# Gate scattering by products of float32r parts instead of whole float32 products, in one layer of a hybrid encoder

## The chip, the cores and the metric

The kernel runs on one core of a Trainium2 chip. The metric is the device time of one execution in microseconds (us), from profiled and timed executions on the chip; lower is better.

## What is computed

One layer over 512 tokens of width 1024, in float32, taken as four blocks of 128 tokens. A projection of the normalised tokens feeds two groups of heads: latent attention (8 heads) and a recurrent RWKV-7 group (8 heads). Their outputs go through an output projection and are added to the tokens. Then comes the part that matters here, a retrieval over 16384 single-neuron experts, each with a row u and a row v of 1024 numbers:

```python
q = (hb @ w_pq).reshape(TOK_BLOCK, PEER_HEADS, 2, PEER_DHALF)
s = jnp.einsum('thpd,hpnd->thpn', q, sub_keys)          # two halves, 128 keys each
s1, i1 = lax.top_k(s[:, :, 0], 16); s2, i2 = lax.top_k(s[:, :, 1], 16)
...                                                     # best 16 of the 256 sums
gate = jax.nn.softmax(top_s, axis=-1)                   # expert index = i1 * 128 + i2
act = jax.nn.gelu(jnp.einsum('thkd,td->thk', expert_u[idx], hb))
out = jnp.einsum('thk,thkd->td', gate * act, expert_v[idx])
```

Every token has 8 heads of 16 experts, so 128 slots, each with i1, i2 and a gate.

## The kernel before

**Stages.** The first 750 us hold the layer's mixing part, in lanes of stages that run side by side, and for each block a stage `back`: output projection (`out_proj`, L784), normalisation (`norm_ffn`, L801), key scores and best 16 (`retrieve`, L837) and the list of experts with its gates (`route`, L862). Blocks 1 and 2 are routed together, block 3 last.

**Experts in two ways.** Blocks 0 and 3 are *gathered* (`experts`, L969): for each of the 128 slots an indirect DMA fetches one row of u or v per token into one of four buffers `ga`, and VectorE multiplies it (L988 for u, L991 for v): 128 u steps and 128 v steps per block, 512 in all. Block 3's steps need the `idx` tile that block 3's `route` writes in L960. Blocks 1 and 2 are *dense* (`dense`, L1052): for their 256 tokens the core goes through all 128 tiles of 128 experts. `up(e)` multiplies the tokens by a tile of u and applies gelu; `down(e)` multiplies the activations by the gates (L1134) and then by a tile of v, adding into four PSUM banks for all 128 tiles (L1138 with whole float32 products, L1149 with float32r parts).

**Gates.** `down` needs the gates as a dense table `G`: for each i2 (partition), token and i1 one number. `gate_half` (L1028) makes it for one half of the i1 values at a time, in 32 iterations of 8 tokens. Slots lie on the partitions. Per iteration VectorE writes B, a one-hot of i1 (L1035), and multiplies it by the gates (L1036); ScalarE writes A, a one-hot of i2 (8 instructions in L1039, one in L1040); TensorE multiplies A by B, 8 products of 128x128 by 128x64 (L1043); ScalarE copies the result into `G` (L1048). B has four buffers, tag "x", which the v halves of L1146 share; A has two. The first half is made before `down(0)`, with the 16 calls `up(12)` to `up(27)` emitted between its iterations; all 32 iterations write into each part of `G`, so `down(0)` follows the last. The second half is emitted between `down(48)` and `down(63)`, two iterations per tile. Tiles run 16 ahead in `up`, in a fixed set of activation buffers; `up(28)` reuses the room of earlier tiles.

**Splitting.** `split` (L1061) makes two float32r tiles of a float32 tile: ScalarE copies it (L1063) and VectorE subtracts the copy (L1064). Some of u and v is split, the rest goes through whole float32 products.

**Memory and order.** `dense` closes the stack `last`, which holds the pools `wb` and `psb` of the `back` stages, and opens the pool `d2` on the same side, so in the room that `wb` gives back:

```python
    last.close()
    d2 = ctx.enter_context(tc.tile_pool(name="d2", bufs=1, side="right", reuse_waits="tile"))
```

In the kernel before, the first tiles of `d2` to be written are `dh` and `dl`, the split tokens, for `up(28)`; then its halves of u (`uh`, `ul`). A scheduler decides the order of the instructions on each engine from the order in which they are emitted and from what each depends on; every engine then runs its instructions strictly in that order. The `back` stages are emitted before `dense`, and the gathers after it.

Of the kernel before, what the change touches and what calls it, by code (L numbers as in the profile page):

```python
# [35 lines left out]
# columns of the packed per-channel vectors  # L36
# [7 lines left out]
# columns of the packed per-feature rows  # L44
# [6 lines left out]
# candidate pairs (a, b) of the two sorted lists that can be among the best 16 sums, in order of a * 16 + b:  # L51
# (a, b) has (a + 1) * (b + 1) - 1 pairs before it that are at least as large
# [3 lines left out]
# lanes of stages: buffers, banks and weight tiles (count, width) of each  # L56
# [7 lines left out]
# blocks whose tokens gather their experts' rows, blocks that go through all experts  # L64
# [4 lines left out]
# dense blocks: gates of HALF * 128 experts at a time, in GBUFS tiles of SUB * 128; activations run AHEAD tiles ahead,  # L69
# FIRST of them before the first gates, KEPT more wait in DRAM  # L70
# [6 lines left out]
def u_whole(e):  # L77
    """float32 products of four passes, where the vector engine has no time to split; else three exact parts"""
    return e < 28 or 47 <= e - AHEAD < 64
# [7 lines left out]
def layer_kernel(ctx: ExitStack, tc: tile.TileContext, x, pos, cvec, rvec, w_mla, w_rwkv, w_uq, w_ukv, lora, g2,  # L87
# [5 lines left out]
    # what the last block's tail needs lies apart: its pools outlive those of the other stages  # L93
# [4 lines left out]
    # the tail takes over the buffers of the second lane  # L98
# [41 lines left out]
    # ---------------------------------------------------------------- constants  # L140
# [65 lines left out]
    # rows (beta s | kappa s), columns (alpha t | rho t)  # L206
# [52 lines left out]
    # rotary tables, token-major  # L259
# [50 lines left out]
    def square_sum(src, scr, acc):  # L310
        """the squares go to a tile that is written after them"""
        act(scr, src, AF.Square, accum_out=acc)

    def head_squares(src, n, acc, h0=0):
        """acc[:, h0 + i] = sum of squares of src[:, i, :n]"""
        for i in range(src.shape[1]):
            act(sb([P, QK], "hscr", dt=BF16)[:, :n], src[:, i, :], AF.Square, accum_out=acc[:, h0 + i:h0 + i + 1])

    # ---------------------------------------------------------------- stages
    def norm_in(xt, hT, carry):  # L320
        """channel-major normalized tokens, after the last one of the block before"""
        ss = sb([P, 1], "ss", 2)
        square_sum(xt.rearrange("p (a b) -> p a b", a=KC), hT[:, :, 1:], ss)
        r = rstd(ss, 1, 1.0 / D, EPS, "nx")
        act(xt, xt, AF.Copy, scale=r)
        if carry is None:
            V.memset(hT[:, :, 0:1], 0.0)
        else:
            V.tensor_copy(hT[:, :, 0:1], carry)
        for i in range(2):  # L330
            p = bank()
            for j in range(4):
                nc.tensor.transpose(p[:, j * P:(j + 1) * P], xt[:, (4 * i + j) * P:(4 * i + j + 1) * P], ident)
            for j in range(4):
                act(hT[:, 4 * i + j, 1:P + 1], p[:, j * P:(j + 1) * P], AF.Copy, scale=col("g_mix", 4 * i + j))
            yield
        carry = sb([P, KC, 1], "carry", 2)
        V.tensor_copy(carry, hT[:, :, P:P + 1])
        return carry

    def rwkv_in(b, hT):
        pm = {}
        if b == EARLY:
            # the gather's buffers are idle until the first block's experts are known
            t = [gb([P, D], "ga", GA).rearrange("p (a b) -> p a b", b=P) for _ in range(2)]
            pm = {"k": t[0][:, 0:4], "r": t[0][:, 4:8], "v": t[1][:, 0:4], "x": t[1][:, 4:6]}
        for g, cols in (("x", (12, 13)), ("k", range(4, 8)), ("r", range(4)), ("v", range(8, 12))):
            if b != EARLY:
                pm[g] = sb([P, 4, P], "pm", PM, pool=wa) if len(cols) == 4 else sb([P, 2, P], "px", 2, pool=wa)
            for i, c in enumerate(cols):  # L350
                w = wtile(w_rwkv[c])
                p = bank()
                for kc in range(KC):
                    mm(p[:, :P + 1], w[:, kc, :], hT[:, kc, :], start=kc == 0, stop=kc == KC - 1)
                t = pm[g][:, i, :]
                act(t, p[:, 1:P + 1], AF.Copy, scale=ommu[:, c:c + 1])
                V.scalar_tensor_tensor(t, p[:, 0:P], col("mu", c), t, op0=OP.mult, op1=OP.add)
                yield
        return pm

    def mla(b, hT, yT):
# [31 lines left out]
        # queries  # L393
# [32 lines left out]
        # keys and values  # L426
# [27 lines left out]
        # block-causal attention, four heads at a time  # L454
# [73 lines left out]
    def rwkv_chunks(b, pm):  # L528
# [68 lines left out]
        # bonus weight and gate  # L597
# [8 lines left out]
        # values, token-major  # L606
# [17 lines left out]
        # chunk-local products  # L624
# [12 lines left out]
        # inverse of the unit lower triangular systems: two chunks stacked on the partitions, heads side by side  # L637
# [70 lines left out]
    def rwkv_scan(b, AR, BKt, MT, UV, YF, wc, bv, sg, yT):  # L708
        # the recurrence over chunks
# [48 lines left out]
        # group norm, bonus, gate  # L758
# [65 lines left out]
    def top16(items):  # L824
        """items: (values, indices, source); the chains of several items interleaved"""
# [11 lines left out]
    def retrieve(bs, h2T):  # L837
        """the best TOPK of both halves' keys, per block"""
# [23 lines left out]
    def route(b, tv, ti):  # L862
        yield
        # the lists of indices as steps: what each rank adds to the one before
# [31 lines left out]
        # rank a of the first list from a candidate's place, rank b of the second from its place within the run  # L896
# [130 lines left out]

    def gate_half(dn, g, parts):  # L1028
        """gates of experts i1 * 128 + i2, i1 in one half: [i2, sub, token, i1 of the SUB]; parts: what takes each run
        of subs"""  # L1030
        i1T, i2T, gT = slots
        for t0 in range(0, nd, 8):
            B = dn.tile([P, 8 * HALF], F32, tag="x", name=f"B{g}_{t0}", bufs=XB)
            B = B.rearrange("p (a b) -> p a b", a=8)
            V.tensor_tensor(B, bm(iotap[:, g * HALF:(g + 1) * HALF], 8), bc(i1T[:, t0:t0 + 8], HALF), op=OP.is_equal)  # L1035
            V.tensor_tensor(B, B, bc(gT[:, t0:t0 + 8], HALF), op=OP.mult)  # L1036
            A = dn.tile([P, 8, P], F32, tag="A", name=f"A{g}_{t0}", bufs=2)
# [4 lines left out]
            for j in range(8):  # L1042
                mm(p[:, j * HALF:(j + 1) * HALF], A[:, j, :], B[:, j, :], start=True, stop=True)  # L1043
# [8 lines left out]
    def dense():  # L1052
# [5 lines left out]
        d2 = ctx.enter_context(tc.tile_pool(name="d2", bufs=1, side="right", reuse_waits="tile"))  # L1058
        nt = len(DENSE)

        def split(t, hi, lo):  # L1061
            """two parts of a float32 tile that the one-pass products carry whole"""
# [13 lines left out]
        # room for activations in the buffers of the second lane  # L1076
# [14 lines left out]
        def up(e, keep=False):  # L1091
            """activations of the experts of a tile, for all tokens of these blocks"""
# [91 lines left out]
    # stages of the blocks, emitted in the order in which they would run side by side; what runs in one lane shares  # L1184
    # its buffers
# [101 lines left out]
```

## Time and profile before

| | |
|---|---|
| median of 3 runs | 1783.02 us (1781.82 to 1790.86) |
| span of the profiled execution, first to last instruction | 1781.3 us |
| TensorE matmul busy | 1651.5 us, 93% |
| VectorE busy | 1334.4 us, 75% |
| ScalarE busy | 932.6 us, 52% |
| GpSimd busy | 702.6 us, 39% |

PE is TensorE's matmul row and PEld its weight loads, DVE is VectorE, ACT ScalarE, POOL GpSimd, SP the engine that issues most DMAs. Matmuls overlap one another, so the duration of one is longer than the distance from its start to the next start; rates below are worked out from starts. The span is 1.7 us below the median of the runs; no other time of the profiled execution is given.

### The profile page before, as it was taken

Reading aid. Unit: us, or ns where it says so; the run is one execution under the profiler, and the core shown is the slowest. Engines: PE = TensorE matmul, PEld = TensorE weight load, DVE = VectorE, ACT = ScalarE, POOL = GpSimd, SP = SyncE. Lnnn points to the kernel's source line nnn. Section 1 sums busy time; section 2 is a strip of 40 time slices with the busy share of each in tenths; the row PEclk is TensorE's granted clock in tenths of the full one; section 3 lists DMA queues with packets and bytes.
Section 4 is the critical chain, followed back from the end, with each engine's and each line's share of the span. In section 5 each row is a group of like instructions: output and inputs, shape, how many; then the busy total and the mean of one; then the engine's idle time right before and its main releaser. Section 6 shows DMA issues by size and latency. Waiting matters only on the chain. (4 is left out here: it accounts for less than half of the span.)

```text
span 1781.3 us, 29137 instructions
## 1 busy us (share of the span) xinstructions
PE 1651.5 (93%) x10183; PEld 1394.3 (78%) x10183; DVE 1334.4 (75%) x2987; ACT 932.6 (52%) x2465; POOL 702.6 (39%) x562
## 2 busy tenths in 40 slices
PE   7999999998999998788997899999999999999987
PEld 6897799787867987567995577888777778888864
DVE  3412414775586789887789789998887799999898
ACT  5656454644545332367774334444768645445443
POOL 1001100244554444454443253334455446356453
PEclk9998999997697999988999999999989999999999
DMA  7634565596689988789997799998989999999988
GB/s 272 196 122 135 164 233 194 203 337 223 213 309 329 324 321 294 290 283 310 364 331 250 258 359 352 359 355 325 327 312 319 312 343 351 366 318 371 346 293 330
DMA packets 154866, 520.71 MB, mean 292 GB/s; under 512 B 17312, under 2 KB 24096, under 8 KB 154720
## 3 DMA queue, kind: packets, MB, share of 16 engines
q0 software_dynamic: 73728, 268.47, 43.1%
q1 hardware_dynamic: 80992, 250.39, 39.6%
q8 instruction: 80, 1.31, 0.3%
q14 instruction: 66, 0.54, 0.1%
HBM read 508.96 MB, written 9.83 MB: 291 GB/s over the span
## 5 line engine op out<-in xcount | busy, mean ns | idle before, releaser
L978 POOL DMA_INDIRECT ga<-in_expert_v_dram,idx x256 | 352.3, 1376 | 381.7 <-DVE acc L991 285.5
L978 POOL DMA_INDIRECT ga<-in_expert_u_dram,idx x256 | 299.8, 1171 | 372.0 <-DVE ga L988 257.5
L991 DVE SCALAR_TENSOR_TENSOR acc<-ga,dots,acc 128x1024 f32<-128x1024 f32 x256 | 327.9, 1281 | 65.9 <-DMA ga<-in_expert_v_dram,idx 64.9
L988 DVE SCALAR_TENSOR_TENSOR ga<-ga,h 128x1024 f32<-128x1024 f32 x256 | 311.6, 1220 | 52.3 <-DMA ga<-in_expert_u_dram,idx 52.1
L1149 PE MATMUL po<-xh,t 128*128 128x512 f32 x880 | 307.7, 407 | 12.7 <-DVE t L1064 5.7
L1117 PE MATMUL ps<-dh,ul 128*128 128x256 f32 x664 | 191.1, 288 | 7.9 <-DVE ul L1064 7.4
L1149 PEld LDWEIGHTS po<-xh,t 128*128 128x128 f32 x880 | 159.6, 192 | 48.6 <-ACT xh L1063 13.2
L1117 PE MATMUL ps<-dh,uh 128*128 128x256 f32 x664 | 189.8, 286 | 6.5 <-ACT uh L1063 6.5
L1149 PE MATMUL po<-xl,t 128*128 128x512 f32 x440 | 179.6, 408 | 14.6 <-DVE xl L1064 14.2
L1117 PE MATMUL ps<-dl,uh 128*128 128x256 f32 x664 | 187.5, 282 | 0.0
L1063 ACT ACTIVATE xh<-v 128x512 fp32r<-128x512 f32 x220 | 134.6, 626 | 96.4 <-PE po L1149 73.9
L1103 PE MATMUL ps<-t,u 128*128 128x256 f32 x720 | 172.6, 393 | 9.1 <-DMA u<-in_expert_ut_dram 8.8
L1103 PEld LDWEIGHTS ps<-t,u 128*128 128x128 f32 x720 | 138.5, 197 | 32.3 <-issue 6.3
L1064 DVE TENSOR_TENSOR xl<-v,xh 128x512 fp32r<-128x512 f32 x220 | 147.7, 690 | 16.2 <-ACT xh L1063 15.7
L1043 PEld LDWEIGHTS ps<-B,A 128*128 128x128 f32 x1024 | 131.3, 204 | 35.3 <-ACT ge L951 10.6
L1039 ACT ACTIVATE A<-iotap,slots 128x128 f32<-128x128 f32 x512 | 156.1, 395 | 0.0
L1043 PE MATMUL ps<-B,A 128*128 128x64 f32 x1024 | 131.5, 285 | 23.6 <-DVE B L1036 10.4
L1063 ACT ACTIVATE uh<-u 128x512 fp32r<-128x512 f32 x166 | 98.5, 625 | 83.8 <-PE ps L1117 52.0
L1117 PEld LDWEIGHTS ps<-dh,ul 128*128 128x128 f32 x664 | 126.4, 190 | 17.3 <-DVE ul L1064 13.4
L1117 PEld LDWEIGHTS ps<-dh,uh 128*128 128x128 f32 x664 | 126.4, 190 | 17.1 <-ACT uh L1063 10.0
L1117 PEld LDWEIGHTS ps<-dl,uh 128*128 128x128 f32 x664 | 126.4, 190 | 3.5 <-issue 0.7
L848 PE MATMUL ps<-h2T,wst 128*128 128x128 f32 (+1 forms) x768 | 125.1, 318 | 3.1 <-DMA wst<-in_w_pq_dram 3.1
(402 smaller groups left out, 2924.1 us busy)
## 6 DMA issues: line engine op xcount, KB each, us to landing
u<-in_expert_ut_dram SPq DMA_DIRECT2D x128, 512.0 KB, 6.7
v<-in_expert_v_dram SPq DMA_DIRECT2D x128, 512.0 KB, 6.6
wst<-in_w_rwkv_dram SPq DMA_DIRECT2D x56, 512.0 KB, 4.4
wst<-in_w_pq_dram SPq DMA_DIRECT2D x48, 512.0 KB, 6.7
wst<-in_w_o_dram SPq DMA_DIRECT2D x24, 512.0 KB, 5.2
wst<-in_w_mla_dram SPq DMA_DIRECT2D x16, 336.0 KB, 3.9
t<-in_x_dram SPq DMA_DIRECT2D x8, 512.0 KB, 4.6
wst<-in_w_ukv_dram SPq DMA_DIRECT2D x16, 256.0 KB, 3.5
```

The source lines that it names most:

```text
L848: mm(p[:, :nb * P], w[:, kc, :], h2T[:, kc, :], start=kc == 0, stop=kc == KC - 1)
L978: G.indirect_dma_start(out=t, out_offset=None, in_=table, in_offset=bass.IndirectOffsetOnAxis(ap=idx[:, j:j + 1], axis=0))
L988: V.scalar_tensor_tensor(u, u, 1.0, h2, op0=OP.mult, op1=OP.mult, accum_out=dots[:, j:j + 1])
L991: V.scalar_tensor_tensor(acc, row_of(expert_v, j), dots[:, j:j + 1], acc, op0=OP.mult, op1=OP.add)
L1039: act(A[:, j, :], iotap, AF.Abs, scale=-1.0, bias=i2T[:, t0 + j:t0 + j + 1])
L1043: mm(p[:, j * HALF:(j + 1) * HALF], A[:, j, :], B[:, j, :], start=True, stop=True)
L1063: act(hi, t, AF.Copy)
L1064: V.tensor_tensor(lo, t, hi, op=OP.subtract)
L1103: mm(p, u[:, kc, :], hd[kc // 2][:, kc % 2, :], start=kc == 0, stop=kc == KC - 1)
L1117: mm(p, a[:, k, :], h[:, kc, :], start=kc + i == 0, stop=kc == KC - 1 and i == 2)
L1149: mm(po[i][n], ww[:, i * P:(i + 1) * P], vv, start=e + k == 0, stop=e == P - 1 and k == 2)
```

## The change

The gates are split once, at the first call of `gate_half`, into two float32r tiles of 128x256 in the pool `d2`. Per iteration there are two tiles B: VectorE writes the one-hot of i1 into one of them and multiplies it by the high and by the low part. A and both B are float32r, and each of the 8 products becomes two, accumulated in PSUM. The other lines of the diff remove comments.

```diff
+    gparts = []
+
     def gate_half(dn, g, parts):
         i1T, i2T, gT = slots
+        if len(gparts) == 0:
+            gparts.extend(pools["d2"].tile([P, nd], F32R, name=f"g{n}") for n in "hl")
+            act(gparts[0], gT, AF.Copy)
+            V.tensor_tensor(gparts[1], gT, gparts[0], op=OP.subtract)
         for t0 in range(0, nd, 8):
-            B = dn.tile([P, 8 * HALF], F32, tag="x", name=f"B{g}_{t0}", bufs=XB)
-            B = B.rearrange("p (a b) -> p a b", a=8)
-            V.tensor_tensor(B, bm(iotap[:, g * HALF:(g + 1) * HALF], 8), bc(i1T[:, t0:t0 + 8], HALF), op=OP.is_equal)
-            V.tensor_tensor(B, B, bc(gT[:, t0:t0 + 8], HALF), op=OP.mult)
-            A = dn.tile([P, 8, P], F32, tag="A", name=f"A{g}_{t0}", bufs=2)
+            Bs = [dn.tile([P, 8 * HALF], F32R, tag="x", name=f"B{n}{g}_{t0}", bufs=XB) for n in "hl"]
+            Bh, Bl = (B.rearrange("p (a b) -> p a b", a=8) for B in Bs)
+            V.tensor_tensor(Bl, bm(iotap[:, g * HALF:(g + 1) * HALF], 8), bc(i1T[:, t0:t0 + 8], HALF), op=OP.is_equal)
+            V.tensor_tensor(Bh, Bl, bc(gparts[0][:, t0:t0 + 8], HALF), op=OP.mult)
+            V.tensor_tensor(Bl, Bl, bc(gparts[1][:, t0:t0 + 8], HALF), op=OP.mult)
+            A = dn.tile([P, 8, P], F32R, tag="A", name=f"A{g}_{t0}", bufs=2)
...
             for j in range(8):
-                mm(p[:, j * HALF:(j + 1) * HALF], A[:, j, :], B[:, j, :], start=True, stop=True)
+                for i, B in enumerate((Bh, Bl)):
+                    mm(p[:, j * HALF:(j + 1) * HALF], A[:, j, :], B[:, j, :], start=i == 0, stop=i == 1)
...
         d2 = ctx.enter_context(tc.tile_pool(name="d2", bufs=1, side="right", reuse_waits="tile"))
+        pools["d2"] = d2
```

## Rows read from the trace of the kernel before

**Rows 1.** First product of `down`'s gates, timeline of DVE.
```profile
952.98 1.61 DVE L1134 TENSOR_TENSOR q<-q,G 128x256 f32<-128x256 f32 x3
```

**Rows 2.** Windows: length; busy us of PE, PEld, DVE, ACT, POOL; PEclk, DMA.
```profile
752.00:953.00 201.00, 179.03 (x1147) 159.68 (x1145) 170.62 (x443) 149.99 (x400) 90.18 (x78) 0.91 0.89 313
953.00:1781.00 828.00, 763.76 (x4280) 632.29 (x4280) 736.79 (x1175) 416.49 (x943) 386.52 (x283) 0.98 0.91 329
1237.00:1420.00 183.00, 170.20 (x920) 140.49 (x919) 145.62 (x207) 136.09 (x377) 100.09 (x80) 0.94 0.89 312
...
957.00:996.00 39.00, 27.67 (x109) 15.88 (x107) 33.57 (x90) 5.85 (x13) 10.49 (x7) 0.91 0.62 203
```

**Rows 3.** Groups of DVE, 953 us to the end: gather steps.
```profile
L991 DVE SCALAR_TENSOR_TENSOR acc<-ga,dots,acc 128x1024 f32<-128x1024 f32 x158 | 202.5, 1282 | 30.0 <-DMA ga<-in_expert_v_dram,idx 29.3
L988 DVE SCALAR_TENSOR_TENSOR ga<-ga,h 128x1024 f32<-128x1024 f32 x128 | 156.1, 1220 | 14.1 <-DMA ga<-in_expert_u_dram,idx 14.1
```

**Rows 4.** Groups of ACT, then of DVE, 752 to 953 us.
```profile
L1039 ACT ACTIVATE A<-iotap,slots 128x128 f32<-128x128 f32 x272 | 82.9, 392 | 0.0
L1040 ACT ACTIVATE A<-A 128x1024 f32<-128x1024 f32 x33 | 34.7, 1053 | 0.3
L1048 ACT ACTIVATE G<-ps 128x512 f32<-128x512 f32 x32 | 18.9, 590 | 18.9 <-PE ps L1043 18.8
...
L1035 DVE TENSOR_TENSOR B<-iotap,slots 128x512 f32<-128x512 f32 x32 | 21.7, 685 | 6.7 <-PE ps L1043 6.6
L1036 DVE TENSOR_TENSOR B<-B,slots 128x512 f32<-128x512 f32 x32 | 21.6, 686 | 0.3
```

**Rows 5.** Weight loads by form, whole span: count, busy us, mean ns, idle before.
```profile
L1043 PEld LDWEIGHTS ps<-B,A 128*128 128x128 f32 x1024 | 131.3, 204 | 35.3 <-ACT ge L951 10.6 <-ACT A L1040 9.4 <-issue 7.6
L1117 PEld LDWEIGHTS ps<-dl,uh 128*128 128x128 f32 x664 | 126.4, 190 | 3.5 <-issue 0.7
...
L909 PEld LDWEIGHTS <-t 128*128 128x128 bf16 x64 | 5.3, 99 | 7.1 <-DVE t L925 4.1 <-DVE B L1035 0.3 <-issue 0.2
```

**Rows 6.** Timeline of PE: start us, us to the end of the last.
```profile
743.32 0.61 PE L909 MATMUL ps<-identb,t 128*128 128x128 bf16 x8
743.76 3.67 PE L1103 MATMUL ps<-t,u 128*128 128x256 f32 x16
747.27 2.25 PE L909 MATMUL ps<-identb,t 128*128 128x128 bf16 x16
...
829.71 1.89 PE L1043 MATMUL ps<-B,A 128*128 128x64 f32 x16
831.44 1.04 PE L809 MATMUL ps<-ident,t 128*128 128x128 f32 x8
...
1457.07 0.28 PE L1117 MATMUL ps<-dh,ul 128*128 128x256 f32 x1
...
1457.90 0.28 PE L1117 MATMUL ps<-dh,uh 128*128 128x256 f32 x1
```

**Rows 7.** Timeline of the SP queue, 943 us: load of tile 28 of u.
```profile
943.30 0.37 SPq L1099 DMA_DIRECT2D u<-in_expert_ut_dram  x1
```

**Rows 8.** Timeline of ACT around the first write into `d2`.
```profile
995.69 0.28 ACT L960 ACTIVATE idx<-ps 128x128 int32<-128x128 f32 x1 [3.39 <-PE ps L947]
995.86 2.18 ACT L1063 ACTIVATE dh<-t 128x512 fp32r<-128x512 f32 x4
997.94 1.14 ACT L1063 ACTIVATE uh<-u 128x512 fp32r<-128x512 f32 x2
```

**Rows 9.** L796's DVE starts for blocks 0 and 3, and L960, L819 by line.
```profile
204.63 0.69 DVE L796 TENSOR_TENSOR t<-t,ps 128x512 f32<-128x512 f32 x1 [0.95 <-PE ps L792]
...
800.39 0.68 DVE L796 TENSOR_TENSOR t<-t,ps 128x512 f32<-128x512 f32 x1
...
L960 ACT ACTIVATE idx<-ps x2: 268/272/277, 338.2 to 995.7; 128x128 int32<-128x128 f32 x2
...
L819 SPq DMA_DIRECT2D h2r<-t x2: 327/327/327, 242.8 to 841.6; - x2
```

## Prediction

> **What bounds the kernel now.** I read the windows first, then the timelines of the engines around the gates, then the groups. From 953 us, when the first product of activations and gates starts [rows 1], to the end, PE is busy 764 of 828 us and DVE 737 [rows 2]: two engines near their limits, with the tiles of `down` and `up` on the one and 286 of the 512 gather steps, at some 1.25 us each, on the other [rows 3]. Neither alone sets the end, so a delay that hits both adds up in full, and relief for one gives back only a part.
>
> The gates lie in two stretches. In the first, 752 to 953 us, the reader is to see ACT: one iteration costs it 8 x 0.305 (82.9 us over 272) + 1.05 + 0.59 = 4.08 us [rows 4], so the 32 iterations take at least 131 us by ACT alone. The stretch lasts 201 us because the 16 calls of `up` and block 3's `back` stage run in it as well. In the second, 1237 to 1420 us, PE is busy 170 of 183 us and DVE 146 [rows 2]. The chain of the second stretch is mixed; PE's and DVE's orders lock into each other there.
>
> **The change part by part.**
>
> *Products.* Before, a whole float32 product is two instructions (1024 for 512 products [rows 5]); after, it is two products of float32r, one instruction each (the split lines show one each). The count stays 1024. Now their pace: sixteen take from 829.71 to 831.44 us, 108 ns each, at 64 columns; at 256 columns sixteen whole ones take from 743.76 to 747.27, 219 ns each [rows 6]. A quarter of the columns would be 55 ns if columns set the pace, so at 64 columns something else does: the weight load. It is 128x128 of four bytes in both kernels, and its mean is 190 ns for float32r as against 204 for L1043's and 99 for bf16 [rows 5]. A float32r product of 256 columns starts 119 ns after the one before (seven in 0.83 us [rows 6]), so one of 64 takes no more than that. Between 55 ns (eight bf16 products in 0.44 us [rows 6]) and 119 I take 108, since the load is as long as the float32 one: PE gains nothing. Bounds for 512 products of one half: 27 us less, 6 us more.
>
> The Trainium skill, in "FP8 and Floating Point Precision", section "TensorE Precision Notes", says that a true float32 product makes four passes through the array; by passes alone the two one-pass products would halve the 55 us of PE per half of the gates. The rows at 64 columns speak against it, as said.
>
> *DVE.* Per iteration one more multiplication of 128x512, at 0.686 us [rows 4]: 32 x 0.686 = 22 us in each half. In the first half an iteration then has 3 x 0.686 = 2.06 us on DVE beside 4.08 us on ACT, which hides it: 0. In the second DVE has 183 - 146 = 37 us idle [rows 2], so most of the 22 us fits, but xl, on which L1149 waits, stands behind it in DVE's order. Bounds 0 and 22; I take 8, nearer to hidden, as there is more idle time than work.
>
> *Buffers.* Tag "x" still has four buffers, and an iteration now takes two. B can run two iterations ahead instead of four; in the second half it alternates with the v halves. ACT's two buffers of A already hold an iteration to two ahead, so I price this at nothing by itself; without that cover DVE would stop at each B, and gather steps behind it too. It belongs to the 22 us above.
>
> *The split of the gates*, one ACT copy and one DVE subtraction of 128x256, is under 1 us. But where its two tiles lie is the largest term. They are tiles of `d2`, whose room is that of the pool `wb`, and `wb` serves block 3's `back` stage until its list of experts is done. Is a tile of `d2` held until then? Before, the first are `dh` and `uh`, for tile 28 of u. That tile was requested at 943.30 us [rows 7]; between 957 and 996 us ACT is busy 5.9 of 39 us and PE 27.7 [rows 2], so there was every room to begin. Yet `dh` is written at 995.86 us, in the instruction behind block 3's last step, `idx` at 995.69 [rows 8]. I read this as the scheduler placing nothing of `d2` before all of `wb` is free. In the kernel before, this costs little, as only tile 28 waits. In the changed one the gates' parts wait, with them every Bh and Bl, so every product of the first half, `G`, and `down(0)`. Only A (two iterations) and the one-hots run ahead.
>
> When is block 3 done without gates beside it? From its first L796 (800.4 us) to `idx` (995.7) it takes 195 us; block 0 took 134 us (204.6 to 338.2) [rows 9]. The gates leave its way, 131 us of ACT, 55 of PE and 43 of DVE [rows 4], and so do the nine tiles of `down` that now come later. I take block 0's pace and 14 us for an earlier start: 800 - 14 + 134 = 920 us, bounds 900 and 996. The 16 `up` calls (16 x 3.5 us [rows 6]) move ahead of that, and `up(28)` has no room before `down`, so PE has little to do while the gates are made: 55 us of products in 131 us. The gates then end at 920 + 131 = 1051 us instead of 953: 98 us later, bounds 78 and 174.
>
> What comes back: the gathers don't wait. In 98 us, at 828/286 = 2.9 us a step [rows 2, 3], they get 34 steps ahead, which takes 34 x 1.25 = 42 us from DVE later on. PE, busy 92% of the same stretch, is not relieved. Bounds 0 and 42; I take 25.
>
> *Sum*, against the span of 1781.3: + 98 (first half late) - 25 (gathers ahead) + 8 (DVE in the second half) + 0 (products) = 1862; the runs' median lies 1.7 us over the span, so **1864 us**, 4.5% slower than 1783. From the bounds: 78 - 42 gives 1819, 174 + 22 gives 1979.
>
> **The rivals.** About 0.5%, 9 us, is what a measurement of this kernel can tell from no change.
>
> 1. *No hold.* The parts are written in time, since `dh` was late only because the scheduler ranked `up(28)` low. Then only DVE and the buffers cost: 0 to 44 us, some 15: 1798 us. For it: the code asks for reuse by tile, and ranking can't be excluded. Against it: the idle ACT and PE [rows 2], and that `dh` comes right behind `idx`.
>
> 2. *A short hold.* Only the tiles whose room the parts take count. The parts would lie next to block 3's token tile, which is stored by L819 at 841.6 us [rows 9]. Gates from about 850: 850 + 131 = 981, 28 later, less 7, plus 8: 1812 us. Against it: the same two rows.
>
> 3. *Faster.* Float32r weights load as fast as bf16 ones. This decides when the products of L1043 start well under 100 ns apart and the first L1036 stays before 800 us. The second half, with PE at 170 of 183 us, gains 512 x (108 - 55) ns = 27 us, the first nothing, as ACT sets it: 1781 - 27 + 8 + 2 = 1764 us. Against it: 190 ns against 99 [rows 5]. The Trainium skill has the rule that speaks for it, in "TensorE: Matmul & The Clock Gate", section "Weight-path perf modes — Fast Weight Load (FWL) and DoubleRow": the fast load is on for 128 weights of a type that is not FP32. By that rule float32r might qualify; the trace does not agree, the float32r loads of L1117 being as long as float32 ones.
>
> **How the numbers follow.** The full hold 0.74, with a range of its own of 1819 to 1950; no hold 0.12; short hold 0.07; faster 0.05; 0.02 for the rest. The range of 80%, 1795 to 1950, takes in the full hold but for its slowest end, the short hold and the upper half of no hold. Faster by over 0.5%: 0.05 and 0.01 from no hold with a luckier order, 0.06. Within 0.5% (1774 to 1792): a third of no hold and some of the rest, 0.05. Slower: 0.89.
>
> **What the profile will show.** If right: the first L1036-like product of B by a part starts after block 3's `idx`, which itself is done well before 996 us; nearly all `up` products to tile 27 lie before the gates; PE is busy under half of a stretch of about 130 us in which ACT is over nine tenths busy; L1043's count is 1024, its pace near 108 ns and its loads near 190 ns; the first L1134-like product starts at 1030 to 1090 us. DVE shows 64 more products of 128x512. More gather steps than 226 lie before that first product.
>
> It goes wrong if the parts are written before block 3 is done (rivals 1 and 2), if block 3 is not quicker without the gates beside it (towards 1950), or if the scheduler, whose order I can't derive from the trace, moves work into the hole on PE that I take to be empty.

## The result and the profile after

The changed kernel takes 1977.96 us (median of four, 1971.83 to 1988.05); the kernel before took 1782.42 us (median of four) beside it. The ratio is 1.1104, 95% interval 1.1043 to 1.1164: slower, as forecast, but by 11.0% and not by 4.5%, and 28 us above the range.

The page of the kernel after, its first two parts: the same 10183 products on PE now keep it busy for 1731 us instead of 1652 us, in a span that is 200 us longer.

```profile
span 1981.6 us, 29363 instructions
PE 1730.6 (87%) x10183; PEld 1458.0 (74%) x10183; DVE 1388.4 (70%) x3052; ACT 944.3 (48%) x2466; POOL 701.0 (35%) x562
...
PE   7999999999999885551878778999989888999998
...
DVE  3413226755767898678988877999988888656665
...
POOL 1001001446454434446655555455555552000000
PEclk9989999976989997785777789999987788999999
```

A hole on PE (5551 in slices 16 to 19), a slow clock beside it and again in slices 30 to 34, and at the end six slices in which POOL does nothing: the gathers have run out, and PE is full to the end (324 of 332 us) with DVE busy for 212.

The times that answer to [rows 1, 9] (by line: count, shortest, median and longest duration, first and last start):

```profile
L1144 DVE TENSOR_TENSOR q<-q,G x23: 581/605/618, 1138.3 to 1930.2; 128x256 f32<-128x256 f32 x23
...
L960 ACT ACTIVATE idx<-ps x2: 269/274/278, 344.6 to 941.7; 128x128 int32<-128x128 f32 x2
...
L819 SPq DMA_DIRECT2D h2r<-t x2: 326/326/326, 249.7 to 818.5; - x2
...
L796 DVE TENSOR_TENSOR t<-t,ps x2: 681/681/681, 791.7 to 805.1; 128x512 f32<-128x512 f32 x2
```

ACT's timeline at the first write into `d2`, which answers to [rows 8]:

```profile
941.69 0.28 ACT L960 ACTIVATE idx<-ps 128x128 int32<-128x128 f32 x1 [15.81 <-PE ps L947]
941.87 0.41 ACT L1036 ACTIVATE gh<-slots 128x256 fp32r<-128x256 f32 x1
942.17 2.18 ACT L1073 ACTIVATE dh<-t 128x512 fp32r<-128x512 f32 x4
```

The high parts of the gates are written right behind block 3's last step, though the token tile that the rival of a short hold names was stored from 818.5 us (L819) and ACT worked 16 of the 142 us before. The hold that was forecast is there. The first product of gates and activations follows at 1138.3 us, 185 us later than before.

Windows, as in [rows 2]: the wait, the first half of the gates, the stretch between, the second half, the rest.

```profile
800.00:942.00 142.00, 55.98 (x346) 48.39 (x344) 108.24 (x338) 16.16 (x40) 76.19 (x61) 0.68 0.87 303
942.00:1138.00 196.00, 156.60 (x792) 138.90 (x792) 165.30 (x236) 133.08 (x345) 108.97 (x86) 0.77 0.83 280
1138.00:1427.00 289.00, 264.02 (x1397) 209.73 (x1397) 256.68 (x403) 110.95 (x222) 148.24 (x99) 0.96 0.93 340
1427.00:1650.00 223.00, 191.60 (x881) 156.10 (x881) 181.74 (x245) 136.23 (x376) 120.30 (x95) 0.81 0.85 297
1650.00:1981.60 331.60, 324.29 (x1942) 287.20 (x1940) 212.46 (x359) 170.86 (x333) 5.33 (x3) 0.99 0.56 186
```

Two stretches are long: the first half takes 196 us where ACT works 133, and the second 223 us, 40 more than before [rows 2]. In neither is one engine full; both have a low granted clock (0.77 and 0.81). Of the 119 us by which the span exceeds the forecast of 1862, 87 lie before the first product of gates and activations: 22 before the gates start (942 us, not 920) and 65 in the first half (196 us, not 131). The other 32 lie behind it, where the forecast had 17 us less than before and the kernel took 15 more.

Groups of the first half, as in [rows 4] (count, busy us, mean ns, idle before and its releasers):

```profile
L1113 PE MATMUL ps<-t,u 128*128 128x256 f32 x256 | 80.2, 483 | 1.4 <-ACT G L1057 1.4
L1047 ACT ACTIVATE A<-iotap,slots 128x128 fp32r<-128x128 f32 x256 | 78.0, 391 | 0.0
...
L1052 PE MATMUL ps<-Bl,A 128*128 128x64 f32 x256 | 71.5, 314 | 20.3 <-DVE Bl L1044 20.2
...
L988 DVE SCALAR_TENSOR_TENSOR ga<-ga,h 128x1024 f32<-128x1024 f32 x45 | 54.6, 1222 | 24.9 <-DMA ga<-in_expert_u_dram,idx 24.9
L991 DVE SCALAR_TENSOR_TENSOR acc<-ga,dots,acc 128x1024 f32<-128x1024 f32 x42 | 53.8, 1281 | 5.3 <-DMA ga<-in_expert_v_dram,idx 4.9
...
L1044 DVE TENSOR_TENSOR Bl<-Bl,gl 128x512 fp32r<-128x512 f32 x32 | 22.0, 686 | 0.0
```

The 256 products of L1113 are the 16 calls of `up` that the prediction had moved ahead; they did not move. And DVE carries 87 gather steps, 108 us, between the passes that make B. PE waits for these passes 34 us in all (total us, times, longest):

```profile
PE ps L1052 <- DVE Bl L1044: 20.2, 17, 3.2
PE ps L1052 <- DVE Bh L1043: 13.9, 6, 4.4
```

PE's timeline has the pace of the products, which answers to [rows 6]:

```profile
999.53 0.28 PE L1052 MATMUL ps<-Bl,A 128*128 128x64 f32 x1
999.64 0.28 PE L1052 MATMUL ps<-Bh,A 128*128 128x64 f32 x1
999.75 0.28 PE L1052 MATMUL ps<-Bl,A 128*128 128x64 f32 x1
```

They start 111 ns apart, with the granted clock at 1.00 (2.4 GHz) from 999.6 to 1002.9 us. From 991.8 to 993.4 us it is 0.50 (1.2 GHz), and the same products start 213 ns apart; in the four us before, PE had stood 0.84 us for A and 0.43 us for Bl.

### The profile page after: what moved, and what is told of

Read it like the earlier page. It is cut to its first block, busy times and chain, and to the rows that moved or that the text cites. A ratio compares the mean times of both kernels' runs of the same rounds, so it can differ in the third digit from the quotient of the medians.

```text
span 1981.6 us, 29363 instructions
## 1 busy us (share of the span) xinstructions
PE 1730.6 (87%) x10183; PEld 1458.0 (74%) x10183; DVE 1388.4 (70%) x3052; ACT 944.3 (48%) x2466; POOL 701.0 (35%) x562
## 4 chain that ended last, share of the span: by engine, by line
PE 47%; DMA 22%; issue 12%; DVE 9%; POOL 7%; ACT 2%; POOLq 0%; DVEq 0%; SPq 0%; ACTq 0%
DMA ga<-in_expert_v_dram,idx 13%; PE po L1159 12%; PE ps L1127 10%; DMA ga<-in_expert_u_dram,idx 7%; POOL ga L978 7%; PE ps L354 5%; PE ps L1113 3%; DVE acc L991 2%; DVE ga L988 2%; PE ps L848 1%; PE ps L674 1%; DMA u<-in_expert_ut_dram 1%; PE ps L692 1%; PE ps L690 1%; PE ps L365 1%
## 5 line engine op out<-in xcount | busy, mean ns | idle before, releaser
L1113 PE MATMUL ps<-t,u 128*128 128x256 f32 x720 | 210.3, 456 | 9.7 <-DMA u<-in_expert_ut_dram 7.7
L1113 PEld LDWEIGHTS ps<-t,u 128*128 128x128 f32 x720 | 165.9, 235 | 42.1 <-issue 7.4
L1074 DVE TENSOR_TENSOR ul<-u,uh 128x512 fp32r<-128x512 f32 x166 | 113.2, 693 | 83.2 <-ACT uh L1073 57.4
L1073 ACT ACTIVATE uh<-u 128x512 fp32r<-128x512 f32 x166 | 102.5, 628 | 143.2 <-PE ps L1127 128.7
L1052 PE MATMUL ps<-Bl,A 128*128 128x64 f32 x512 | 139.9, 310 | 31.1 <-DVE Bl L1044 31.0
L1052 PE MATMUL ps<-Bh,A 128*128 128x64 f32 x512 | 142.0, 313 | 21.9 <-DVE Bh L1043 18.0
L1047 ACT ACTIVATE A<-iotap,slots 128x128 fp32r<-128x128 f32 x512 | 156.0, 393 | 0.0
L848 PE MATMUL ps<-h2T,wst 128*128 128x128 f32 (+1 forms) x768 | 128.6, 325 | 20.5 <-DMA wst<-in_w_pq_dram 20.4
L1052 PEld LDWEIGHTS ps<-Bl,A 128*128 128x128 f32 x512 | 115.3, 225 | 36.3 <-DVE Bl L1044 34.9
L1052 PEld LDWEIGHTS ps<-Bh,A 128*128 128x128 f32 x512 | 114.9, 224 | 31.8 <-ACT A L1048 14.1
```

The source lines that it names most:

```text
L848: mm(p[:, :nb * P], w[:, kc, :], h2T[:, kc, :], start=kc == 0, stop=kc == KC - 1)
L1047: act(A[:, j, :], iotap, AF.Abs, scale=-1.0, bias=i2T[:, t0 + j:t0 + j + 1])
L1073: act(hi, t, AF.Copy)
L1074: V.tensor_tensor(lo, t, hi, op=OP.subtract)
L1113: mm(p, u[:, kc, :], hd[kc // 2][:, kc % 2, :], start=kc == 0, stop=kc == KC - 1)
```

## The experiments

Stage times are starts of instructions in the profiled executions, in us; "list" is the last step of block 3's list (L960), "first" is the span from the first to the last eviction of the first half (L1048 of the kernel before), "product" the first product of gates and activations, "second" the evictions of the second half. e8_after_nogather and e9_before_nogather ran once each and have no ratio.

| kernel | ratio to before (95%) | list | first | product | second | span |
|---|---|---|---|---|---|---|
| before | 1 | 995.7 | 766 to 949 | 953 | 1239 to 1418 | 1781 |
| after | 1.1104 (1.1043 to 1.1164) | 941.7 | 951 to 1135 | 1138 | 1427 to 1650 | 1982 |
| e1_hold | 1.0789 (1.0739 to 1.0840) | 938.6 | 944 to 1108 | 1121 | 1410 to 1586 | 1920 |
| e2_free | 1.0423 (1.0389 to 1.0457) | 990.1 | 767 to 986 | 989 | 1276 to 1499 | 1847 |
| e3_ups_first | 1.1210 (1.1172 to 1.1248) | 962.4 | 971 to 1156 | 1162 | 1448 to 1665 | 1992 |
| e4_dve | 1.0134 (1.0104 to 1.0165) | 993.1 | 772 to 948 | 954 | 1234 to 1438 | 1802 |
| e5_prod | 1.0078 (1.0035 to 1.0121) | 1004.2 | 772 to 957 | 960 | 1245 to 1438 | 1801 |
| e6_pair | 1.0202 (1.0152 to 1.0252) | 997.1 | 766 to 951 | 955 | 1233 to 1442 | 1802 |
| e14_both | 1.0263 (1.0215 to 1.0311) | 995.4 | 769 to 964 | 967 | 1249 to 1468 | 1819 |
| e7_bf16 | 1.0009 (0.9976 to 1.0042) | 998.0 | 774 to 926 | 930 | 1219 to 1392 | 1779 |
| e10_packed | 1.0177 (1.0129 to 1.0224) | 1017.6 | 767 to 933 | 935 | 1242 to 1409 | 1795 |
| e12_pairs | 0.9925 (0.9896 to 0.9955) | 1001.6 | 767 to 919 | 919 | 1224 to 1379 | 1768 |
| e13_prod_bf16 | 0.9899 (0.9870 to 0.9929) | 997.3 | 765 to 916 | 917 | 1224 to 1374 | 1761 |
| e11_null | 0.9999 (0.9968 to 1.0030) | 992.6 | 767 to 949 | 952 | 1231 to 1415 | 1777 |
| e8_after_nogather | - | 806.5 | 814 to 961 | 962 | 1214 to 1395 | 1726 |
| e9_before_nogather | - | 861.0 | 738 to 915 | 915 | 1168 to 1329 | 1655 |

Ratios are turned into us with 1780, about what the kernel before took in these runs.

**The hold alone: e1_hold.** The kernel before, with the gates read through a float32 copy that lies in `d2`.

```diff
+        if len(gparts) == 0:
+            gparts.append(pools["d2"].tile([P, nd], F32, name="gc"))
+            act(gparts[0], gT, AF.Copy)
...
-            V.tensor_tensor(B, B, bc(gT[:, t0:t0 + 8], HALF), op=OP.mult)
+            V.tensor_tensor(B, B, bc(gparts[0][:, t0:t0 + 8], HALF), op=OP.mult)
```

> The kernel before, with one edit: the first call of gate_half copies the gates into a float32 tile of d2, and the multiplication of B reads that copy. Products, DVE work and buffers stay as before. Theory (the hold): the copy is written only once block 3's list of experts is done, about 942 us, the first half of the gates starts there and the time is 1930 to 1970 us, most of the 200 us. Rival (DVE and buffers): the place of the gates' parts costs nothing by itself, and the time is 1775 to 1795 us.

It took 1919.22 us, 140 us more than before: a little under the range of the theory, and the rival is out by far. One copy in the wrong pool, with the products and DVE's two passes as before, brings most of the loss. Its windows are the first half, the second half and the rest:

```profile
939.00:1121.00 182.00, 138.71 (x768) 125.58 (x768) 137.96 (x190) 131.82 (x345) 106.56 (x81) 0.81 0.84 289
...
1410.00:1586.00 176.00, 161.91 (x894) 133.71 (x894) 138.56 (x195) 136.13 (x378) 92.56 (x75) 0.97 0.89 312
1586.00:1919.00 333.00, 321.87 (x1930) 283.46 (x1928) 238.95 (x384) 169.04 (x331) 60.71 (x29) 1.00 0.65 227
```

The first product comes 168 us later than before; from there to the end it takes 798 us instead of 828. So 30 us come back, near the 25 that were forecast, with 309 gather steps before the first product instead of 226. PE is full to the end from 1586 us on (322 of 333 us). The first half takes 182 us with two passes an iteration, so the third pass is not what makes it longer than 131. PE waits only 8 us for B here; ACT waits once for 12 us in front of a gather's gelu (L994) that needs the last step of a group on DVE. What fills the rest of this stretch was not told apart.

**Everything but the hold: e2_free.** The changed kernel with both parts made in `route`, in the slots' own room.

```diff
-            gparts.extend(pools["d2"].tile([P, nd], F32R, name=f"g{n}") for n in "hl")
-            act(gparts[0], gT, AF.Copy)
-            V.tensor_tensor(gparts[1], gT, gparts[0], op=OP.subtract)
+            gparts.extend((gT, slots[3]))
...
+        V.tensor_tensor(slots[3][:, o:o + P], p[:, 2 * P:3 * P], slots[2][:, o:o + P], op=OP.subtract)
```

> The changed kernel, but its two parts lie in the slots' own tiles of the pool wm and are made in route, from the bank (the low part and the first list of indices as bf16, to fit): nothing of the gates lies in d2. Theory (the hold): the first half starts before 800 us as in the kernel before; what is left is the second half's loss of some 34 us, so 1800 to 1830 us. Rival (DVE and buffers): an iteration stays as slow wherever the parts lie, and the time is 1930 to 1980 us.

1853.98 us, 75 us more than before. The first half starts at 767 us again, so the hold is gone, but what is left is more than twice the 34 us that the theory named, and above its range. With e1_hold's 140 the sum is 215, near the 197 of the whole change: the two prices nearly add up.

**Is it the calls of `up` in the stretch? e3_ups_first.** The changed kernel with these calls written ahead.

```diff
-        for e in range(FIRST):
-            up(e)
-        for i, _ in enumerate(gate_half(dn, 0, [whole])):
-            for e in range(FIRST + i * rest // n, FIRST + (i + 1) * rest // n):
-                up(e, e >= AHEAD)
+        for e in range(FIRST + rest):
+            up(e, e >= AHEAD)
+        for _ in gate_half(dn, 0, [whole]):
+            pass
```

> The changed kernel, with all calls of up for tiles 0 to 27 written ahead of the first half of the gates instead of between its iterations. Theory (two banks): the 16 calls stood in the stretch because gates and up take turns at two banks; now they run while the gates wait, PE has 80 us less to do in the stretch of 196 us and the time is 1880 to 1930 us. Rival (DVE sets the stretch: each B stands behind gather steps): the stretch stays near 190 us and the time within 15 us of 1978.

1995.47 us, 17 us more than the changed kernel: my theory fell. The calls left the stretch, the list came 20 us later, and the stretch stayed at 185 us with much less for PE to do. The waits of 971 to 1161 us (total us, times, longest) name what sets it:

```profile
ACT G L1057 <- PE ps L1052: 58.1, 29, 6.1
...
PE ps L1052 <- DVE Bl L1044: 48.6, 29, 4.1
```

and DVE's timeline, with the place of Bl in its order:

```profile
1052.99 0.08 DVE L988 DVE_READ_ACCUMULATOR ga<-ga,h 128x1 f32 x1
1054.36 1.22 DVE L988 SCALAR_TENSOR_TENSOR ga<-ga,h 128x1024 f32<-128x1024 f32 x1 [1.29 <-DMA ga<-in_expert_u_dram,idx]
1055.51 0.08 DVE L988 DVE_READ_ACCUMULATOR ga<-ga,h 128x1 f32 x1
1055.51 0.69 DVE L1044 TENSOR_TENSOR Bl<-Bl,gl 128x512 fp32r<-128x512 f32 x1
1056.12 1.22 DVE L988 SCALAR_TENSOR_TENSOR ga<-ga,h 128x1024 f32<-128x1024 f32 x1
```

Bl stands behind a gather step that waits 1.29 us for its row, and PE behind Bl, ACT's eviction behind PE. DVE was busy for 172 of these 190 us. The run leaves one rival standing: PE's granted clock is 0.51 in this stretch, as against 0.77 in the changed kernel, so the products that are left are slower. The next run settles it.

**The gather steps taken out: e8_after_nogather and e9_before_nogather.** The changed kernel and the kernel before, each with `for g in range(0)` in `experts`.

> The changed kernel without the gather steps of blocks 0 and 3, so their experts are left out. Theory (in the first half the gates stand behind gather steps in DVE's order): the start of the gates still waits for block 3's list, but the 32 iterations take 131 to 150 us instead of 185, near ACT's 131. Rival (PE with the 16 calls of up and a low granted clock sets the stretch): 170 us or more.

> The kernel before without the gather steps of blocks 0 and 3, so their experts are left out; it stands beside e8_after_nogather. Theory (the hold costs little when block 3 is not slowed by gather steps, and DVE's passes are free then): 40 to 70 us below e8_after_nogather's 1728, 1660 to 1690 us. Rival (the 200 us come from PE and ACT): 1530 to 1600 us.

One run each: 1727.56 us, and 1657.00 us, a little under its range. In the changed kernel the list is done at 806.5 us, not 941.7, the parts are written at 806.7, and the 32 evictions take from 814 to 961.5 us, 148 us and not 185: at the upper edge of the theory's range. From e8_after_nogather come block 3's first L796, its list with the write of the high parts, and PE's waits from 806.5 to 962 us:

```profile
721.99 0.69 DVE L796 TENSOR_TENSOR t<-t,ps 128x512 f32<-128x512 f32 x1 [5.79 <-PE ps L792]
...
806.48 0.28 ACT L960 ACTIVATE idx<-ps 128x128 int32<-128x128 f32 x1 [8.55 <-PE ps L947]
806.66 0.41 ACT L1036 ACTIVATE gh<-slots 128x256 fp32r<-128x256 f32 x1
...
PE ps L1052 <- DVE Bl L1044: 2.0, 1, 2.0
...
PE ps L1052 <- DVE Bh L1043: 1.7, 1, 1.7
```

PE's waits for Bl and Bh fall from 34 to 4 us, which is nearly all of the 37 us that the evictions gain; the granted clock, 0.81, is near the 0.77 of the changed kernel, so the clock is not what set the stretch. The difference of the two kernels without gathers is 71 us, 47 of them in the first half (first product at 962 as against 915 us). So about 126 of the 197 us are there only while there are gather steps.

The stages show how. From its first L796 to its list block 3 takes 195 us in the kernel before and 150 in the changed one; without gather steps it takes 130 and 84. So the gather steps cost block 3 some 65 us in either kernel, and the gates beside it some 45 with or without them. The steps hold block 3 back, and with it the release, and then they stand between the gates' passes. Without the steps their transfers are gone as well, and no run parted DVE's order from the transfers. The traces show some of both: in block 3's part of the changed kernel PE waits 19 us for the weights `w_pq` (L848), and 4 us without the gathers; in the first half of the gates 30 us of DVE's idle time are waits of gather steps for their rows.

**DVE's pass alone: e4_dve.** The kernel before with `V.tensor_tensor(B, B, B, op=OP.max)` behind the multiplication.

> The kernel before, with one more DVE pass over B in every iteration (the larger of B and B, so the values stay). Theory: as the prediction has it, hidden in the first half and partly in the second, 1783 + 8: 1783 to 1800 us. Rival (DVE is the bound): 44 us of DVE add up in full, 1820 to 1830 us.

1803.41 us, 24 us by the ratio. That is between the theory and the rival. By stages the kind is the prediction's: nothing in the first half, 205 us instead of 178 in the second. Of the pass's 22 us there, nothing is hidden: PE waits 18 us for it in the second half, where the trace of the kernel before shows no wait for B.

**The buffers alone: e6_pair.** Two tiles of tag "x" an iteration, with DVE's two passes as before.

```diff
-            B = dn.tile([P, 8 * HALF], F32, tag="x", name=f"B{g}_{t0}", bufs=XB)
+            Bs = [dn.tile([P, 8 * HALF], F32, tag="x", name=f"B{n}{g}_{t0}", bufs=XB) for n in "eg"]
...
-                mm(p[:, j * HALF:(j + 1) * HALF], A[:, j, :], B[:, j, :], start=True, stop=True)
+                mm(p[:, j * HALF:(j + 1) * HALF], A[:, j, :], (E if j == 7 else B)[:, j, :], start=True, stop=True)
```

> The kernel before, but the one-hot rows stay in a tile of tag x of their own and the gates' products go to a second: two of the four buffers an iteration, both held until its last product, with the same two DVE passes. The last of each eight tokens takes the one-hot rows, so its gates are left out. Theory (buffers): e2_free lost 73 us and DVE's pass explains 23 of them, so the buffers cost 30 to 55 us: 1812 to 1838 us. Rival (they cost nothing, as the prediction had it; the loss comes from how the three passes depend on each other): 1775 to 1795 us.

1812.82 us, 36 us by the ratio: the theory's range. In the profiled execution, the fastest of four, the loss lies in the second half: 209 us instead of 178, with PE waiting 24 us for the second tile of B. The first half is level. That it is the v halves, which take buffers of the same tag there, fits this and was not tested by itself.

**The products alone: e5_prod.** A and B as float32r, two products of the same B.

```diff
-                mm(p[:, j * HALF:(j + 1) * HALF], A[:, j, :], B[:, j, :], start=True, stop=True)
+                for i in range(2):
+                    mm(p[:, j * HALF:(j + 1) * HALF], A[:, j, :], B[:, j, :], start=i == 0, stop=i == 1)
```

> The kernel before, with A and B as float32r and two one-pass products of the same B in place of one float32 product; gates come out rounded and doubled (the low part is left out). DVE and buffers are as before. Theory (the load sets the pace): products start 108 to 111 ns apart as in the kernel before, time 1783 +- 10 us. Rival (the pass sets it): some 55 to 60 ns apart, 50 us less of PE, time 1740 to 1765 us.

1795.87 us, 14 us by the ratio (6 to 21). That is 3 us above the theory's 1793. The pace is the theory's: sixteen products with 1.95 us to the end of the last, 111 ns apart, weight loads of 192 ns in the median.

```profile
848.32 1.95 PE L1044 MATMUL ps<-B,A 128*128 128x64 f32 x16
```

That is 3 ns on each of 1024 products, 3 us; the other 11 us are not in the pace, and I had not expected them.

**The order alone: e11_null.** The kernel before with `reversed(range(8))` over an iteration's products.

> The kernel before with the eight products of an iteration written in the opposite order: the same work, another program for the scheduler. It asks whether a few of the 14 us of e5_prod can come from the order alone. Theory (the order alone moves the time by some 10 us): 1790 us or more, or 1770 or less. Rival (it does not): within 5 us of the kernel before.

Level, 0.9999: this change of order does not move the time, so order alone is no ready excuse for e5_prod.

**Short loads: e7_bf16 and e13_prod_bf16.** The first has two bf16 parts made in `route`, one tile of tag "x" for both, A in bf16, and three DVE passes; the second is e5_prod with bf16 for float32r.

```diff
+            B = dn.tile([P, 2 * 8 * HALF], BF16, tag="x", name=f"B{g}_{t0}", bufs=XB)
+            B = B.rearrange("p (a b) -> p a b", a=16)
+            Bh, Bl = B[:, :8], B[:, 8:]
...
-            A = dn.tile([P, 8, P], F32, tag="A", name=f"A{g}_{t0}", bufs=2)
+            A = dn.tile([P, 8, P], BF16, tag="A", name=f"A{g}_{t0}", bufs=2)
```

> Two parts again, but in bf16: the high part of a gate is its bf16 value, the low part the bf16 value of the rest, both made in route in the slots' own room, the one-hot rows and A in bf16 as well, and both products of an iteration share one tile of tag x. Gates keep some 16 bits. No hold, four iterations of buffers as before, DVE one pass more. Theory: bf16 loads take 99 ns as against 190, products start some 55 ns apart, PE does 50 us less, and DVE's pass costs the 23 us of e4_dve or less: 1745 to 1785 us. Rival (DVE sets the end and PE's gain is lost): 1795 to 1810 us.

> e5_prod with bf16 in place of float32r: A and B in bf16 and two products of the same B, DVE's two passes and the buffers' count as in the kernel before; gates come out rounded and doubled. Theory (e7_bf16 is DVE's 23 us and PE's gain set off against each other): products 55 ns apart and a time of 1750 to 1765 us, and with it e5_prod's loss lies in float32r's pace and order, not in writing two products. Rival (two products in one place cost by themselves): 1780 us or more.

1780.54 us, level, and 1762.40 us, 18 us less than before. The first lies at the upper end of its theory's range, the second in it. The products start 30 ns apart, not the 55 of both theories, and the loads take 98 ns. With bf16 two products in place of one gain; e7_bf16 gains on PE too (1594 us busy, and 1581 in e13_prod_bf16, as against 1652) and pays it to DVE's third pass (18 us gained by e13_prod_bf16, 24 lost by e4_dve). So the loss of e5_prod is tied to float32r and not to the writing of two products.

**DVE's passes made cheap: e10_packed and e12_pairs.** e7_bf16 with all operands of the passes 16-bit and with step 1 innermost: eight tokens innermost in B in the one, two in the other. The lines show e12_pairs against e7_bf16.

```diff
-            V.tensor_tensor(Bh, Bl, bc(gh[:, t0:t0 + 8], HALF), op=OP.mult)
+            def pairs(s):
+                return s[:, t0:t0 + 8].rearrange("p (c a) -> p c a", a=2)[:, :, None, :].to_broadcast([P, 4, HALF, 2])
...
+            V.tensor_tensor(Bh, Bl, pairs(gh), op=OP.mult)
...
-                    mm(p[:, j * HALF:(j + 1) * HALF], A[:, j, :], B[:, j, :], start=i == 0, stop=i == 1)
+                    mm(p[:, j * HALF:(j + 1) * HALF], A[:, j, :], B[:, j // 2, :, j % 2], start=i == 0, stop=i == 1)
```

> e7_bf16 with one thing changed: the eight tokens stand innermost in B, with 16-bit iota and indices, so all three operands of each DVE pass over B are 16-bit with step 1 innermost; the products read B with a step of eight elements. Theory: such a pass takes about half of the 0.685 us of e7_bf16's, so the three passes together cost DVE some 1.1 us an iteration, less than the two of the kernel before (1.37 us), and with PE's gain of e7_bf16 the time is 1735 to 1765 us. Rival: the passes stay at 0.685 us, or the strided reads slow the products above 55 ns, and the time is 1775 to 1800 us. The Trainium skill, in VectorE: DVE Perf Modes, section What auto-detection actually checks, asks for step 1 and 16 bits of every tensor for the double rate.

> e10_packed with two tokens innermost in B instead of eight: DVE still sees 16-bit operands with step 1 innermost, and the products read B with a step of two elements, four bytes, instead of eight. Theory: DVE keeps the 0.42 us passes of e10_packed (or slightly more) and the products get back the pace of e7_bf16, some 55 ns apart; then both gains count and the time is 1735 to 1765 us, below the kernel before. Rival (any step above one element slows the product, or pairs are too short for DVE): 1775 to 1810 us.

Groups of e7_bf16, of e10_packed and of e12_pairs (count, busy us, mean ns):

```profile
L1041 DVE TENSOR_TENSOR B<-B,slots 128x512 bf16<-128x512 bf16 x64 | 43.0, 685 | 0.1
```

```profile
L1054 PE MATMUL ps<-B,A 128*128 128x64 bf16 x1024 | 127.0, 294 | 17.8 <-DVE B L1045 8.6 <-DVE B L1046 5.0 <-ACT A L1050 4.0
...
L1045 DVE TENSOR_TENSOR B<-B,slots 128x512 bf16<-128x512 bf16 x64 | 25.5, 419 | 0.3
```

```profile
L1059 PE MATMUL ps<-B,A 128*128 128x64 bf16 x1024 | 43.1, 197 | 32.1 <-ACT A L1055 18.2 <-DVE B L1050 9.1 <-DVE B L1051 3.2
...
L1050 DVE TENSOR_TENSOR B<-B,slots 128x512 bf16<-128x512 bf16 x64 | 25.8, 418 | 0.3
```

PE's rows of products of e10_packed, then of e12_pairs:

```profile
856.03 2.02 PE L1054 MATMUL ps<-B,A 128*128 128x64 bf16 x16
```

```profile
864.34 1.12 PE L1059 MATMUL ps<-B,A 128*128 128x64 bf16 x32
```

In both kernels, a pass of 512 elements falls from 685 to 419 ns. With a step of eight elements the products pay for it: sixteen take 2.02 us, (2.02 - 0.29) / 15 = 115 ns apart, and the time is 1809.41 us, above the rival's range. With a step of two they keep the pace of e7_bf16, 32 in 1.12 us, 30 ns apart, and 1768.78 us is 0.7% below the kernel before, with an interval that excludes no gain. It is the version with both parts of the gates (in bf16, some 16 bits) that beats both kernels, though not by the 15 us and more that were expected: its second half ends 39 us earlier (1379 as against 1418 us) and the rest takes until 1768, with DVE busy for 355 and PE for 339 of the last 389 us.

**Buffers and pass together: e14_both.** e6_pair with `V.tensor_tensor(E, E, E, op=OP.max)` behind its multiplication.

> e6_pair (two tiles of tag x an iteration; the last of each eight tokens takes the one-hot rows, so its gates are left out) with a third DVE pass over the first tile, as the changed kernel has it, still with float32 products. Theory (the two prices stand beside each other, 36 + 24 us): 1830 to 1850 us, and the first half's end late as in e2_free, some 985 us, where neither alone moved it from 953. Rival (the pass hides under the wait for a buffer): 1805 to 1820 us, and e2_free's late first half comes from the float32r products.

1826.78 us, 47 us by the ratio, between the two. That is 13 us less than the two prices together, at the edge of what the three intervals can tell, so at most a small part of the pass hides under the wait for a buffer. The first half ends 14 us late, not 36. The other 28 us of e2_free's 75 come with what e14_both lacks: float32r products, and parts held in the slots' room.

## Why the prediction was right in kind and too small

Right: **the hold**, with its mark (gh 0.18 us behind `idx`); that **float32r gains nothing at 64 columns** (111 ns forecast as 108, loads of 192 ns in the median); that **gathers get ahead** (314 steps before the first product, 226 before the change) and give something back (25 us forecast, 30 in e1_hold). That last number is near by luck: 34 steps ahead were forecast, and 83 came in e1_hold. That the load is what sets the pace of float32r fits bf16, with loads half as long and products 30 ns apart; no run changed the load alone. The rivals of no hold, of a short hold and of a faster kernel are out.

Wrong were the sizes of the sum's terms, each of them measured by itself:

| term of the sum | forecast | measured |
|---|---|---|
| hold: first half late, less what comes back | 98 - 25 = 73 | 140 (e1_hold) |
| DVE's pass | 8 | 24 (e4_dve) |
| two buffers an iteration | 0 | 36 (e6_pair) |
| products | 0 | 14 (e5_prod) |

The four sum to 214 us, and the whole change costs 197. The difference is within what the intervals of the five ratios leave open.

*The hold.* The step that failed is "I take block 0's pace and 14 us for an earlier start: 920 us", and above all "The gates then end at 920 + 131 = 1051 us", which gives the stretch ACT's work and nothing else. Block 3 took 150 us, not 134, and began 9 us early, not 14: the list came at 941.7. The stretch took 196 us, and ACT was busy for 133 of them, not for nine tenths. Block 0 had no gather steps beside it; block 3 has 65 in that time, 81 us of DVE. That 134 comes so near to 150 is luck: without gather steps block 3 takes 84 us (e8_after_nogather). I costed the stretch by its busiest engine and left out that DVE works in one order, in which each pass that makes B stands among gather steps and their waits for rows; without these the evictions take 148 us and not 185. That the 16 calls of `up` "move ahead" failed too, but e3_ups_first shows that it was worth nothing. The first product came 185 us late, outside the bound of 174.

*The buffers.* "I price this at nothing by itself" was the plainest error: 36 us in e6_pair. A's two buffers do not cover for B in the second half, where PE waits 24 us for it.

*DVE's pass.* "Nearer to hidden, as there is more idle time than work" compared sums over 183 us. The idle time was there, but 34 of the 37 us were waits of gather steps for their rows, and the pass did not fill them: PE waits 18 us for it in e4_dve.

*The range.* The sum of the bounds reached 1979 us, which is what came, but by other terms: it had 174 us for the first half and 22 for DVE's pass, with nothing for the buffers. I cut it at 1950 as the slowest end.

What stays open is float32r's own cost: 14 us alone and 28 in the company of the others, of which the pace explains 3. The second half of e5_prod shows a granted clock of 0.90 as against 0.94 [rows 2]; whether that is cause or effect was not told apart.

## What to carry to other kernels

Ask of every new tile whose room it takes over and when that is given back: here one tile in the wrong pool cost 140 us, where the added DVE passes cost 24. Cost a stretch by the order of its engines, not by the busiest: an operation with a little work on a shared engine waits for whatever stands ahead of it, and a buffer taken twice an iteration halves the distance that could hide it. Where a product has few columns, measure the pace of the operand type at that width first: making the operands 16-bit gained what float32r did not.

## What the runs showed of the hardware

- Weight loads of 128x128 take 192 ns in the median for float32r (e5_prod) as for float32 (the kernel before), and 97 ns for bf16 (e12_pairs). Instructions of 64 columns start 111, 108 and 30 ns apart; a float32 product is two of them. The Trainium skill has in "TensorE: Matmul & The Clock Gate", section "Weight-path perf modes — Fast Weight Load (FWL) and DoubleRow", a fast load for 128 weights of a type that is not FP32; the runs agree for bf16, and float32r loads like FP32.
- The step at which a bf16 product reads its moving operand counts: with two elements 30 ns (e12_pairs), with eight 115 ns (e10_packed) for the same 64 columns.
- A DVE multiplication of 128x512, all bf16, takes 685 ns with one operand broadcast along the innermost axis (e7_bf16), and 419 ns with step 1 there (e10_packed, e12_pairs). The Trainium skill, in "VectorE: DVE Perf Modes", section "What auto-detection actually checks", asks for 16 bits and step 1 of every tensor; the runs agree, and a broadcast along an outer axis does no harm.
- PE's granted clock was 0.68 in the hole of the changed kernel, with PE busy for 56 of 142 us, and 0.77 in the stretch behind it, with PE busy for 157 of 196 us; there the products of `up` take 483 ns in the mean, as against 393 over the whole span of the kernel before. The busy share alone does not order the stretches: in e3_ups_first the clock was 0.51 with PE busy for 123 of 190 us.
